# Attention written out for TensorE by groups of key tiles: the sample stream among the first head pair's blocks, and the first output-projection tiles in the last pair

## The chip, the core and the metric

The kernel runs on one core of a Trainium2 chip. The metric is the device time of one execution, in microseconds (us), as the median over runs. Five engines are named as the profile names them: PE (TensorE matmuls; PEld is its weight load), DVE (VectorE), ACT (ScalarE), POOL (GpSimd) and SP (SyncE, which issues the DMA transfers here). Each engine works through its own instructions in the order in which the program put them and waits on semaphores for the others.

## What is computed

Two layers over one prompt of 1024 tokens and a sample stream of 64 tokens with 512 cached keys. Only layer 0 matters here. Its even mixer takes one combined input projection and one output projection around two branches:

```
q, k, v, ga, qi, ki, wi, gb, gc, xin, gz = split(h @ w_in)
score = sum_h wi * relu(qi . ki)                    # the indexer
top_idx = top_k(score, min(256, L // 4))            # per query
p = softmax(q . k[top_idx] / 8);  o = p . v[top_idx]
a_out = o * silu(ga)                                # branch A
b_out = gb * conv3(gc * xin) * silu(gz)             # branch B
x = x + gate * (concat(a_out, b_out) @ w_out)
```

The kernel doesn't gather: a search finds each query's threshold score, a mask turns it into a bias that is added to the logits of all keys, and the softmax runs over all keys of a block.

## The kernel before

**Matmuls.** Every fp32 product is made of three: each operand is split into a high part (`hi`) and a rest (`lo`), and hi x hi, lo x hi, hi x lo are summed. A weight tile of the input projection (128 output channels) takes 8 slices of the inner dimension x 3 products x 3 column chunks (364, 364, 360 of the 1088 tokens), 72 matmuls, here called **steps**: `steps` (L250, its matmul is L262) is a generator that hands out one at a time. Weights come by SP (`w_raw`), ACT makes `w_hi` (L238), and POOL, or for the output projection mostly DVE, makes `w_lo` (L239).

**Masks.** Once the thresholds are known, DVE makes the bias of seven blocks (`mask`, L602 to L607) while PE works on the projection tiles that are still left: 11 of them, `ATTN_TILES` (queries of pairs 1 to 3, `gb` 0 to 3, `ga` 0 to 3). Their results are taken out of PSUM by ACT, and those of `gb` by DVE (L894), which multiplies them into `bo`.

**Attention.** Four head pairs `t`, each with eight blocks `b` of 128 queries (block b sees 128(b+1) keys) and then a sample block (64 queries of both heads in one, 576 keys). One block: logits on PE (L620), a masked maximum on DVE that also moves them to SBUF as `S` (L622), exp and sum on ACT (L625), reciprocal on DVE (L626), scaling on POOL (L627), transposes of `S` on PE by groups of two key tiles x two heads (L650), a split of these into `pth` (ACT, L276) and `ptl` (DVE, L277), and the weighted sum of v on PE (L658). ACT and DVE bring the result into `q` (L662, L722). At a pair's start ACT and POOL split its queries into `qst` (L698, L699). After a pair POOL multiplies `q` by silu(ga) (L912); for pair 3, ACT and DVE do it by chunks (L905, L906).

**What sets the order.** The tile framework orders the instructions of each engine by its own simulated timeline. Into it the kernel ties the projection steps: `BEFORE = 435` steps come ahead of attention, and `pace` drops one or two more behind each logits, weighted-sum and transpose piece (`RATE`). PSUM has eight banks of 512 columns: two for projections (`pj`), three for logits (`lg`), two for transposes (`pt`), one for weighted sums (`av`).

**After attention** the output projection (op, L247) runs over three column chunks x eight tiles of `wo`; it needs `q` and `bo` split into `ah` and `al` (L276, L277), and adds into `x` (loaded by SP).

Of the kernel before, what the change touches and what calls it, by code (L numbers as in the profile page):

```python
# [9 lines left out]
F32 = mybir.dt.float32  # L10
# [7 lines left out]
P = 128  # L18
# [30 lines left out]
ATTN_TILES = [(Q_, 1), (Q_, 2), (Q_, 3), *((GB, t) for t in range(4)), *((GA, t) for t in range(4))]  # L49
# [35 lines left out]
ORDER = [(0, 1, 2, 3, 4, 5, 6, 7)] + [(7, 0, 6, 1, 5, 2, 4, 3)] * 3  # L85


BEFORE = 435
RATE = ((1, 1, 2),) * 4
# [8 lines left out]
class Trunk:  # L98
    def __init__(self, tc, ins, outs):
        self.tc, self.nc = tc, tc.nc  # L100
        self.i, self.o = ins, outs
        self.tags = ["pj"]

# [6 lines left out]
    def bank(self, tag, name):  # L110

        return self.ps.tile([P, 512], F32, tag=tag, name=name, bufs={"pj": 2, "lg": 3, "pt": 2, "av": 1}[tag])
# [137 lines left out]
    def steps(self, w, evac, chunks=range(NCH), n=2, tag="pj"):  # L250
# [3 lines left out]
        for c in chunks:  # L254
            a, b = CHUNKS[c]
            ps = self.bank(tag, "pj")[:, 0:b - a]
# [230 lines left out]
    def topk(self, pool):  # L487
# [11 lines left out]
        self.kneg = kneg = t("kneg")  # L499
# [11 lines left out]
        cv, m, sgn, limx, T, cand, flag = (t(n) for n in ("cv", "m", "sgn", "limx", "T", "cand", "flag"))  # L511
        self.T, self.cv, self.sgn = T, cv, sgn
        junks = [self.cum, pool.tile([P, SEQ], BF, name="junk")]
# [78 lines left out]
    def mask(self, pool, j):  # L592
# [14 lines left out]
        V.tensor_scalar(bi, bi, MASK, None, op0=OP.mult)  # L607


    def softmax(self, slot, lhs, keys, g, n, bias):  # L610

        nc = self.nc
        k, w = cut(n)
        p = self.S[:, slot:slot + n]
        st = self.small.tile([P, 4], F32, tag="sm", name="sm", bufs=8)
        for c in range(k):
            s = slice(c * w, (c + 1) * w)
            pt = self.bank("lg", "logit_ps")
            for i in range(2):
                mm = nc.tensor.matmul(pt[:, 0:w], lhs, keys[i][:, g, s], start=i == 0, stop=i == 1)  # L620
            self.pace(mm.ins, self.rate[0])
            nc.vector.tensor_tensor_reduce(out=p[:, s], in0=pt[:, 0:w], in1=bias[:, s], scale=-0.125,  # L622
                                           scalar=st[:, c - 1:c] if c else 3.0e38, op0=OP.add, op1=OP.min,
                                           accum_out=st[:, c:c + 1])
        nc.scalar.activation(p, p, AF.Exp, scale=-1.0, bias=st[:, k - 1:k], accum_out=st[:, 2:3])  # L625
        nc.vector.reciprocal(st[:, 3:4], st[:, 2:3])  # L626
        nc.gpsimd.tensor_scalar(p, p, st[:, 3:4], 0.0, op0=OP.mult, op1=OP.add)  # L627
        return p

    def weighted(self, pool, ps, g, n, vbase):  # L630

        nc = self.nc
        m = len(ps) * P
        av = self.bank("av", "av")
        nj = (n + P - 1) // P
        step = 512 // m
        for j0 in range(0, nj, step):
            js = range(j0, min(j0 + step, nj))
            full = [j for j in js if (j + 1) * P <= n]
            pt = self.bank("pt", "p_ps")  # L640
            hi = pool.tile([P, 512], F32R, tag="pth", name="pth", bufs=2)
            lo = pool.tile([P, 512], F32R, tag="ptl", name="ptl", bufs=2)
            for part in (full, [j for j in js if j not in full]):
                if not part:
                    continue
                r = min(P, n - part[0] * P)
                for j in part:
                    for i, p in enumerate(ps):
                        o = (j - j0) * m + i * P
                        mm = nc.tensor.transpose(pt[0:r, o:o + P], p[:, j * P:j * P + r], self.ident)  # L650
                if part is full:
                    self.pace(mm.ins, self.rate[2])
                x = slice((part[0] - j0) * m, (part[-1] + 1 - j0) * m)
                self.split(hi[0:r, x], lo[0:r, x], pt[0:r, x])
                for j in part:
                    o = (j - j0) * m
                    for i, t in enumerate((hi, lo)):
                        mm = nc.tensor.matmul(av[:, 0:m], self.vs[0:r, vbase + j, g, :], t[0:r, o:o + m],  # L658
                                              start=j == 0 and i == 0, stop=j == nj - 1 and i == 1)
            self.pace(mm.ins, self.rate[1])  # L660
        low = pool.tile([64, 256], F32, tag="avl", name="avl", bufs=2)
        nc.scalar.activation(low[:, 0:m], av[64:P, 0:m], AF.Copy)  # L662
        return av, low
# [27 lines left out]
    def pair_stack(self, pool, t):  # L691

        nc = self.nc
        st = [pool.tile([P, TC], F32R, tag=f"qst{e}", name="qst") for e in range(2)]
        for a, b in ((0, 512), (512, TC)):
            for e in range(2):
                x, h, l = self.q[64 * e:64 * e + 64, t, a:b], slice(64 * e, 64 * e + 64), slice(64 - 64 * e, P - 64 * e)
                nc.scalar.activation(st[e][h, a:b], x, AF.Copy)  # L698
                nc.gpsimd.tensor_sub(st[e][l, a:b], x, st[e][h, a:b])  # L699
        return st  # L700

    def sample_keys(self, pool):
        for g in range(2):
            for o in range(0, PAST, 256):
                raw = pool.tile([P, 256], F32, tag="ckr", name="ckr", bufs=1)
                self.load(raw, self.i["ck"][g, :, o:o + 256])
                self.split(self.kc[0][:, g, o:o + 256], self.kc[1][:, g, o:o + 256], raw, self.nc.gpsimd)
# [3 lines left out]
    def attend(self, pool, st, t, b):  # L711
        n = P * (b + 1)
        c = slice(b * P, (b + 1) * P)
        if b < 2:
            bias = self.corner[:, 256 - n:256]
        else:
            bias = self.bias[:, SOFF[b - 2]:SOFF[b - 2] + n]
        ps = [self.softmax(self.slot(n), st[e][:, c], self.kp, t // 2, n, bias) for e in range(2)]
        av, low = self.weighted(pool, ps, t // 2, n, 0)
        for e in range(2):  # L720
            s = slice(e * P, (e + 1) * P)
            self.nc.vector.tensor_add(self.q[64 * e:64 * e + 64, t, c], av[0:64, s], low[:, s])  # L722

    def attend_sample(self, pool, st, t):
        both = pool.tile([P, P], F32R, tag="qs", name="qs", bufs=1)
        for e in range(2):
            self.nc.vector.tensor_copy(both[:, e * DEC:(e + 1) * DEC], st[e][:, SO:SO + DEC])
# [34 lines left out]
    def layer0(self):  # L762
# [41 lines left out]
        with ExitStack() as es:  # L804
# [40 lines left out]
            with self.pool("search", "right") as se:  # L845
# [31 lines left out]
                for j in range(NSB):  # L877
                    self.mask(se, j)
# [342 lines left out]
```

## Time and profile before

| | |
|---|---|
| three runs | 1160.75, 1156.42, 1159.66 us; median 1159.66 us |
| the profiled execution, its own time | 1157.27 us (span 1155.5 us) |
| PE busy | 1100.1 us, 95% of the span, mean granted clock 0.983 |
| DVE, ACT, POOL busy | 58%, 45%, 38% |
| first of the 11 attention-phase projection tiles on PE | 344.70 us |
| first logits matmul | 424.81 us |
| end of the 96th matmul of the output projection | 653.7 us |

How to read it: times of a view count from the span's start. The three runs lie within 0.4% of each other, and the profiled execution is at their lower end. [...]

### The profile page before, as it was taken

The page shows a single profiled execution, that of the slowest core. Times are in us where ns is not written, and L with a number is a line of the kernel's source. Part 1 is how long each engine was busy: PE and PEld are TensorE (multiplying, and loading weights), DVE is VectorE, ACT ScalarE, POOL GpSimd, SP SyncE. Part 2 cuts the span into 40 slices and gives each one's busy share as a digit, 9 for nine tenths or more (in the row PEclk, how much of TensorE's full clock was granted, in tenths as well). Part 3 has the DMA queues.
Part 4 walks back from the last instruction along what each step waited for, and adds up shares of the span by engine and source line. Part 5 has one row for each costly group of instructions (what it writes and reads, how often), then busy time and mean ns, then how long its engine had stood idle before and what let it go on. Part 6 is the DMA issues. An engine that isn't in the chain of part 4 may idle for free.

```text
span 1155.5 us, 18886 instructions
## 1 busy us (share of the span) xinstructions
PE 1100.1 (95%) x7255; PEld 1051.7 (91%) x7255; DVE 670.9 (58%) x1657; ACT 516.8 (45%) x976; POOL 442.6 (38%) x454
## 2 busy tenths in 40 slices
PE   4899999999999979999898999999999999999997
PEld 4789689999999968888797999999999999999996
DVE  5712799998886998776666424411186064247134
ACT  5233686856777147777757313511221211135111
POOL 2633223466547165354523136521133211154222
PEclk9999999999999989998999999999999999999999
DMA  9746411211101110000000801011112111131012
GB/s 362 305 156 215 179 29 56 91 40 38 37 19 56 37 46 10 20 1 19 19 1 19 281 2 40 35 55 37 37 57 82 37 37 37 38 109 37 1 65 91
DMA packets 26074, 81.84 MB, mean 71 GB/s; under 512 B 3072, under 2 KB 9984, under 8 KB 23552
## 3 DMA queue, kind: packets, MB, share of 16 engines
q1 hardware_dynamic: 25984, 80.63, 19.8%
q8 instruction: 57, 0.93, 0.3%
q14 instruction: 33, 0.27, 0.1%
HBM read 74.50 MB, written 6.12 MB: 70 GB/s over the span
## 4 chain that ended last, share of the span: by engine, by line
PE 79%; DVE 8%; ACT 5%; issue 3%; POOL 2%; DMA 2%; SPq 0%; POOLq 0%; DVEq 0%; ACTq 0%
PE pj L247 40%; PE op L247 16%; PE pj L262 8%; PE av L658 3%; PE p_ps L650 2%; PE logit_ps L620 2%; PE ada_ps L153 2%; PE score_ps L427 1%; PE sgu_ps L1036 1%; PE first L318 1%; DVE cum L604 1%; PE score_ps L428 1%; POOL w_lo L239 1%; POOL hf L329 1%; ACT S L625 1%
## 5 line engine op out<-in xcount | busy, mean ns | idle before, releaser
L247 PE MATMUL pj<-ah,w_hi 128*128 128x364 f32 (+1 forms) x984 | 326.0, 331 | 1.0 <-ACT w_hi L238 1.0
L247 PE MATMUL pj<-al,w_hi 128*128 128x364 f32 (+1 forms) x984 | 323.8, 329 | 0.0
L247 PE MATMUL pj<-ah,w_lo 128*128 128x364 f32 (+1 forms) x984 | 323.1, 329 | 0.0
L239 POOL TENSOR_TENSOR w_lo<-w_raw,w_hi 128x1024 fp32r<-128x1024 f32 x63 | 159.1, 2527 | 351.2 <-ACT w_hi L238 350.8
L247 PEld LDWEIGHTS pj<-ah,w_hi 128*128 128x128 f32 x984 | 185.0, 188 | 2.0 <-ACT w_hi L238 1.3
L247 PEld LDWEIGHTS pj<-ah,w_lo 128*128 128x128 f32 x984 | 184.8, 188 | 0.3 <-issue 0.2
L247 PEld LDWEIGHTS pj<-al,w_hi 128*128 128x128 f32 x984 | 185.1, 188 | 0.0
L238 ACT ACTIVATE w_hi<-w_raw 128x1024 fp32r<-128x1024 f32 x69 | 72.9, 1058 | 135.7 <-PE pj L247 83.2
L247 PE MATMUL op<-ah,w_lo 128*128 128x448 f32 (+2 forms) x384 | 126.5, 330 | 3.0 <-POOL w_lo L239 3.0
L247 PE MATMUL op<-ah,w_hi 128*128 128x448 f32 (+2 forms) x384 | 127.1, 331 | 0.9 <-ACT ah L276 0.5
L247 PE MATMUL op<-al,w_hi 128*128 128x448 f32 (+2 forms) x384 | 126.4, 329 | 0.7 <-DVE al L277 0.7
L528 DVE TENSOR_SCALAR_CACHE_REDUCE cum<-S,cand 128x512 bf16<-128x512 f32 (+5 forms) x142 | 119.1, 838 | 2.0
L262 PE MATMUL pj<-ah,w_hi 128*128 128x364 f32 (+1 forms) x288 | 96.0, 333 | 6.6 <-DVE bo L894 5.6
L262 PE MATMUL pj<-al,w_hi 128*128 128x364 f32 (+1 forms) x288 | 96.4, 335 | 0.0
L262 PE MATMUL pj<-ah,w_lo 128*128 128x364 f32 (+1 forms) x288 | 95.7, 332 | 0.0
L976 DVE SCALAR_TENSOR_TENSOR x<-op,mod,x 128x192 f32<-128x192 f32 (+2 forms) x64 | 30.4, 497 | 104.9 <-PE op L247 102.5
L555 ACT ACTIVATE junk<-S,cand 128x896 bf16<-128x896 f32 (+2 forms) x78 | 77.7, 996 | 24.3 <-DVE m L558 20.5
L627 POOL TENSOR_SCALAR S<-S,sm 128x384 f32<-128x384 f32 (+8 forms) x68 | 50.4, 748 | 87.2 <-DVE sm L626 64.9
L247 PEld LDWEIGHTS op<-ah,w_lo 128*128 128x128 f32 x384 | 73.0, 190 | 5.5 <-POOL w_lo L239 3.3
L247 PEld LDWEIGHTS op<-ah,w_hi 128*128 128x128 f32 x384 | 73.0, 190 | 3.5 <-ACT ah L276 0.9
L247 PEld LDWEIGHTS op<-al,w_hi 128*128 128x128 f32 x384 | 73.0, 190 | 3.3 <-DVE al L277 1.1
L984 POOL TENSOR_TENSOR acc<-acc,sq 128x448 f32<-128x448 f32 (+2 forms) x40 | 39.2, 979 | 94.4 <-ACT sq L982 93.6
(242 smaller groups left out, 2001.3 us busy)
## 6 DMA issues: line engine op xcount, KB each, us to landing
w_raw<-in_w SPq DMA_DIRECT2D x53, 512.0 KB, 3.4
ada<-in_ada_w SPq DMA_DIRECT2D x19, 1024.0 KB, 9.1
w_raw<-in_wo SPq DMA_DIRECT2D x16, 512.0 KB, 3.5
x<-in_x SPq DMA_DIRECT2D x8, 544.0 KB, 6.6
bo<-in_ada_w SPq DMA_DIRECT2D x4, 1024.0 KB, 6.9
x<-in_x SPq DMA_DIRECT2D x1, 1792.0 KB, 9.5
out_y<-x SPq DMA_DIRECT2D x1, 1792.0 KB, 6.6
x<-in_x SPq DMA_DIRECT2D x1, 1536.0 KB, 9.4
```

The source lines that it names most:

```text
L153: nc.tensor.matmul(pt[32 * g:32 * g + 32, 0:P], self.cs[:, kt, :], raw(kt)[:, g * P:(g + 1) * P], start=kt == 0, stop=kt == KT - 1, tile_p ...
L238: nc.scalar.activation(hi, raw, AF.Copy)
L239: (nc.gpsimd if lo_eng == "pool" else nc.vector).tensor_sub(lo, raw, hi)
L247: last = self.nc.tensor.matmul(ps, wt[:, kt, :], at[:, kt, c0:c1], start=n == 0, stop=n == len(mms) - 1)
L262: self.nc.tensor.matmul(ps, wt[:, kt, :], at[:, kt, a:b], start=kt == 0 and i == 0, stop=kt == KT - 1 and i == 2)
L528: V.tensor_scalar(junks[0][:, 0:SW[j]], self.S[:, span(j)], thr, 0.0, op0=OP.is_lt, op1=OP.add, accum_out=col(cv, j))
L555: nc.scalar.activation(junks[1][:, 0:SW[j]], self.S[:, span(j)], AF.Sign, scale=-1.0, bias=col(cand, j), accum_out=col(cv, j))
L620: mm = nc.tensor.matmul(pt[:, 0:w], lhs, keys[i][:, g, s], start=i == 0, stop=i == 1)
L627: nc.gpsimd.tensor_scalar(p, p, st[:, 3:4], 0.0, op0=OP.mult, op1=OP.add)
L658: mm = nc.tensor.matmul(av[:, 0:m], self.vs[0:r, vbase + j, g, :], t[0:r, o:o + m], start=j == 0 and i == 0, stop=j == nj - 1 and i == 1)
L976: nc.vector.scalar_tensor_tensor(x[:, t, a:b], ps[:, a:b], self.mod[l][:, 16 + t, j:j + 1], x[:, t, a:b], op0=OP.mult, op1=OP.add)
L984: nc.gpsimd.tensor_add(acc, acc, sq)
```

## The change

PE's order in the attention phase is no longer left to the framework: within `manual_schedule` for PE it is the program's own order. `attend` writes it out by **slots**; a slot is one group of two key tiles (four for a sample block), 88 in all. Each slot issues the transposes of its group, the logits of whatever block falls due (a block's last logits come `LEAD = 4` slots ahead of its first transposes), some projection steps (`FILL`: 2.9, 5.0, 5.5, 6.0 per slot in pairs 0 to 3, and 3.6 once the output projection has begun), and the weighted sum of the group two slots back (`LAG = 2`). The same matmuls are issued as before, in another order.

Besides:

- The four sample blocks stand among pair 0's blocks. All of pair 3's blocks but four then lie behind `half()`, from which on the slots are filled with the output projection's tiles 0 and 1 of chunk 0 (48 matmuls, `early_out`).
- `BEFORE` is 459. Ahead of attention the projection's results rotate over five banks instead of two; in attention `lg` has two banks, and weighted sums have two (`av` and `x`).
- The masks are emitted in the attention pool, and the scratch `cum` of `mask` shares the buffer of `ga`.
- silu(ga) is made as ga x (1 + tanh(ga/2)) with the half in the softmax's scale: tanh on ACT by chunks, a product on DVE, and a multiplication into `q` at the end of the pair (POOL; DVE for pair 3).
- The next pair's queries are split in the middle of the pair before; the sample keys and both sample query tiles ahead of attention.
- The output projection takes its inner slices in the order 4 to 7, 0 to 3 in layer 0.

```diff
+FILL = (2.9, 5.0, 5.5, 6.0, 3.6)
+LEAD, LAG = 4, 2
-ORDER = [(0, 1, 2, 3, 4, 5, 6, 7)] + [(7, 0, 6, 1, 5, 2, 4, 3)] * 3
-BEFORE = 435
-RATE = ((1, 1, 2),) * 4
+ORDER = [(0, 1, 2, 3, "s0", "s1", 6, "s2", "s3", 7, 5, 4)] + [(0, 7, 1, 6, 2, 5, 3, 4)] * 2 + [(0, 3, 1, 2, 4, 7, 5, 6)]
+BEFORE = 459
+OUT_KTS = (4, 5, 6, 7, 0, 1, 2, 3)
...
+    def attend(self, pool, through, half):
...
+        for g in range(int(ahead[0][0]), len(slots) + LAG):
+            if 0 <= g < len(slots):
+                it, js = slots[g]
+                waiting.append((it, js, self.transposes(pool, it, js)))
...
+                if js[0] == 0 and it in ((0, ORDER[0][-3]), (1, ORDER[1][3]), (2, ORDER[2][3])):
+                    self.queries(pool, it[0] + 1)
+            while ahead and ahead[0][0] <= g and self.room(ahead[0][1:]):
+                _, it, e, c = ahead.pop(0)
+                self.logits(it, e, c)
...
+            credit += FILL[-1 if self.halved else pair[min(max(g, 0), len(slots) - 1)]]
+            while credit >= 1:
+                credit -= 1
+                next(self.side, None)
+            if waiting and (len(waiting) > LAG or g >= len(slots)):
+                it, js, parts = waiting.pop(0)
+                self.weighted(pool, it, js, parts)
+                if (js[-1] + 1) * P >= self.keys_of(it):
+                    if it[1] == ORDER[it[0]][-1]:
+                        through(it[0])
+                    elif it == (3, ORDER[3][3]):
+                        half()
...
-                self.cum = se.tile([P, SEQ], BF, name="cum")
+                self.cum = ap.tile([P, 2 * TC], BF, tag="ga", name="cum")
...
+                        g = ga[t][:, cols(c)]
+                        nc.scalar.activation(g, ps, AF.Tanh, scale=0.5)
+                        nc.vector.scalar_tensor_tensor(g, g, 1.0, ps, op0=OP.add, op1=OP.mult)
...
-                        while kind == GA and self.done <= t:
+                        while kind == GA and not (self.last if t == 3 else self.done >= t):
                             yield
...
+                self.side = chain(tiles(), self.early_out(fetch))
+                self.tags = ["pj", "pj", "lg", "lg", "lg"]
+                with self.tc.manual_schedule(engines={mybir.EngineType.PE}):
+                    for j in range(NSB):
+                        self.mask(j)
+                    for _ in range(BEFORE):
+                        next(self.side)
+                    self.attending, self.tags = True, ["pj"]
+                    self.queries(ap, 0)
+                    self.sample_keys(ap)
+                    self.attend(ap, through, half)
```

Three places in the order show it. The first is DVE at the end of the masks (`bias`) and the start of attention (`S<-logit_ps`). Before, the last mask rows are mixed with results of `gb` (`bo`), and the first logits follow:

```order
L604 TENSOR_TENSOR_SCAN cum_1909<-ones_77,cv_1973,bias_600 128x576
L607 TENSOR_SCALAR bias_600<-bias_600 128x1024
L605 SCALAR_TENSOR_TENSOR bias_600<-cum_1909,bias_600 128x576
L894 TENSOR_TENSOR bo_604<-bo_604,pj_4385 128x364
L606 SCALAR_TENSOR_TENSOR bias_600<-S_603,T_1977,bias_600 128x576
L607 TENSOR_SCALAR bias_600<-bias_600 128x576
L894 TENSOR_TENSOR bo_604<-bo_604,pj_4411 128x360
L622 ISA S_603,sm_4457<-logit_ps_4458,corner_601 128x128
```

In the changed kernel the same place reads:

```order
L618 SCALAR_TENSOR_TENSOR cum_3874<-ones_77,cv_1909,bias_600 128x576
L983 TENSOR_TENSOR bo_604<-bo_604,pj_4381 128x364
L621 TENSOR_SCALAR bias_600<-bias_600 128x1024
L619 SCALAR_TENSOR_TENSOR bias_600<-cum_3874,bias_600 128x576
L620 SCALAR_TENSOR_TENSOR bias_600<-S_603,T_1911,bias_600 128x576
L983 TENSOR_TENSOR bo_604<-bo_604,pj_4407 128x360
L621 TENSOR_SCALAR bias_600<-bias_600 128x576
L997 SCALAR_TENSOR_TENSOR ga_4464<-ga_4464,pj_4439 128x364
L659 ISA S_603,sm_4501<-logit_ps_4502,corner_601 128x128
```

All masks still stand ahead of the first logits; new between them is the first product of `ga`, whose buffer `cum` has to leave first.

The second is PE at the end of pair 2. Before, the sample block's weighted sum (`av` of 128 columns) stands there with the next pair's logits and with two projection steps:

```order
L650 MATMUL p_ps_6258<-ident_69,S_603 128x128 x4
L262 MATMUL pj_6232<-al_65,w_hi_5642 128x364
L262 MATMUL pj_6232<-ah_64,w_lo_5643 128x364
L658 MATMUL av_6182<-pth_6184,vs_1905 128x128
...
L620 MATMUL logit_ps_6511<-kp0_1903,qst_6213 128x384
L620 MATMUL logit_ps_6511<-kp1_1904,qst_6213 128x384
L658 MATMUL av_6182<-ptl_6202,vs_1905 128x128
L650 MATMUL p_ps_6274<-ident_69,S_603 128x128 x4
```

In the changed kernel pair 3's first logits (`st1`) stand in a slot like any other, with steps of the projection in each:

```order
L275 MATMUL pj_6132<-ah_64,w_lo_5393 128x360
L702 MATMUL av_6244<-pth_6162,vs_1905 128x256
L702 MATMUL av_6244<-ptl_6163,vs_1905 128x256
...
L684 MATMUL p_ps_6249<-ident_69,S_603 128x128 x4
L658 MATMUL logit_ps_6259<-kp0_1903,st1_5016 128x128
L658 MATMUL logit_ps_6259<-kp1_1904,st1_5016 128x128
L275 MATMUL pj_6272<-ah_64,w_hi_5896 128x364
L275 MATMUL pj_6272<-al_65,w_hi_5896 128x364
L275 MATMUL pj_6272<-ah_64,w_lo_5897 128x364
```

What moved is the sample block (now in pair 0) and the projection steps, which are spread over the slots.

The third is ACT at the end of attention, where the output projection's third and fourth weight tiles (`w_hi`) are made. Before, they stand behind the splits (`ah`) that follow the last sample block:

```order
L662 ACTIVATE avl_6794<-av_6768 64x128
L276 ACTIVATE ah_64<-q_602 128x384
L276 ACTIVATE ah_64<-q_602 128x256
L238 ACTIVATE w_hi_6958<-w_raw_6956 128x1024
L238 ACTIVATE w_hi_6964<-w_raw_6962 128x1024
```

In the changed kernel they stand behind the last block's result (`cs` now holds what `avl` held):

```order
L289 ACTIVATE pth_6892<-p_ps_6891 128x256
L707 ACTIVATE cs_81<-av_6886 64x256
L289 ACTIVATE ah_64<-q_602 128x384
L289 ACTIVATE ah_64<-q_602 128x256
L249 ACTIVATE w_hi_6972<-w_raw_6970 128x1024
L249 ACTIVATE w_hi_6978<-w_raw_6976 128x1024
```

What moved here is little: the third tile is still made behind the last splits, but tiles 0 and 1 of chunk 0 have been multiplied by then.

## Rows read from the trace of the kernel before

**Rows 1.** The page: busy time of each engine, share of the span.

```profile
PE 1100.1 (95%) x7255; PEld 1051.7 (91%) x7255; DVE 670.9 (58%) x1657; ACT 516.8 (45%) x976; POOL 442.6 (38%) x454
```

**Rows 2.** Windows: length, then busy us of PE, PEld, DVE, ACT, POOL; PE's clock.

```profile
344.70:653.70 309.00, 285.95 (x1735) 266.29 (x1734) 228.53 (x638) 192.36 (x399) 136.76 (x131) 0.95 0.11 36
350.00:400.00 50.00, 50.00 (x303) 50.00 (x302) 40.92 (x117) 24.66 (x45) 24.70 (x30) 1.00 0.15 51
412.00:416.00 4.00, 3.91 (x14) 3.92 (x15) 4.00 (x3) 0.00 (x0) 3.85 (x3) 0.57 0.08 29
424.80:440.00 15.20, 12.94 (x72) 11.13 (x70) 12.28 (x54) 13.63 (x36) 10.96 (x15) 0.89 0.17 53
566.00:583.00 17.00, 13.01 (x62) 11.32 (x61) 8.70 (x29) 11.90 (x25) 8.98 (x9) 0.70 0.10 32
583.00:611.00 28.00, 27.86 (x195) 26.89 (x195) 18.14 (x58) 16.98 (x39) 6.69 (x9) 1.00 0.00 1
611.00:644.00 33.00, 28.02 (x158) 25.59 (x157) 22.28 (x44) 21.73 (x45) 9.89 (x3) 0.95 0.30 104
```

**Rows 3.** Waits of PE, 344.7 to 653.7: total us, times, longest.

```profile
PE pj L262 <- DVE bo L894: 5.6, 2, 3.3
PE p_ps L650 <- DVE ptl L277: 5.1, 6, 3.7
PE logit_ps L620 <- DVE sm L622: 3.3, 4, 2.2
PE op L247 <- POOL w_lo L239: 3.0, 1, 3.0
```

**Rows 4.** Timeline of DVE in the mask phase: start, us, instruction.

```profile
391.50 0.62 DVE L606 SCALAR_TENSOR_TENSOR bias<-S,T,bias 128x384 bf16<-128x384 f32 x1
394.54 2.77 DVE L606 SCALAR_TENSOR_TENSOR bias<-S,T,bias 128x512 bf16<-128x512 f32 x1
...
402.58 0.29 DVE L607 TENSOR_SCALAR bias<-bias 128x640 bf16<-128x640 bf16 x1
...
407.04 2.49 DVE L607 TENSOR_SCALAR bias<-bias 128x768 bf16<-128x768 bf16 x1
...
424.85 0.31 DVE L607 TENSOR_SCALAR bias<-bias 128x576 bf16<-128x576 bf16 x1
```

**Rows 5.** Timeline of POOL in the mask phase.

```profile
393.89 2.87 POOL L239 TENSOR_TENSOR w_lo<-w_raw,w_hi 128x1024 fp32r<-128x1024 f32 x1 [9.58 <-ACT w_hi L238]
405.89 3.42 POOL L239 TENSOR_TENSOR w_lo<-w_raw,w_hi 128x1024 fp32r<-128x1024 f32 x1 [9.13 <-ACT w_hi L238]
409.39 8.92 POOL L699 TENSOR_TENSOR qst<-q,qst 64x512 fp32r<-64x512 f32 x4
```

**Rows 6.** Lines by form, POOL, 440 to 620: count, busy us, mean ns, idle before.

```profile
L239 POOL TENSOR_TENSOR w_lo<-w_raw,w_hi 128x1024 fp32r<-128x1024 f32 x4 | 9.5, 2386 | 10.8 <-ACT w_hi L238 10.7
L699 POOL TENSOR_TENSOR qst<-q,qst 64x512 fp32r<-64x512 f32 x6 | 7.7, 1285 | 3.6 <-DVE sm L626 2.2 <-ACT qst L698 1.1
```

**Rows 7.** Lines by form, the softmax's chain and the splits, 440 to 620.

```profile
L622 DVE CUSTOM_DVE_ANT_0 S<-logit_ps,bias,sm 128x512 f32<-128x512 f32 x8 | 6.0, 750 | 1.9 <-PE p_ps L650 1.6
L625 ACT ACTIVATE S<-S,sm 128x1024 f32<-128x1024 f32 x8 | 9.2, 1148 | 1.2 <-DVE sm L622 1.2
L626 DVE RECIPROCAL sm<-sm 128x1 f32<-128x1 f32 x57 | 9.0, 160 | 13.0 <-ACT S L625 12.5
L627 POOL TENSOR_SCALAR S<-S,sm 128x1024 f32<-128x1024 f32 x8 | 9.0, 1123 | 27.2 <-DVE sm L626 27.1
L662 ACT ACTIVATE avl<-av 64x256 f32<-64x256 f32 x30 | 11.4, 381 | 8.7 <-PE av L658 8.1
L722 DVE TENSOR_TENSOR q<-av,avl 64x128 f32<-64x128 f32 x60 | 16.8, 280 | 7.9 <-ACT avl L662 7.3
L238 ACT ACTIVATE w_hi<-w_raw 128x1024 fp32r<-128x1024 f32 x4 | 4.2, 1050 | 0.1
```

**Rows 8.** The page's DMA issues: count, KB each, median us to landing.

```profile
x<-in_x SPq DMA_DIRECT2D x1, 1792.0 KB, 9.5
```

More of the change, by code (lines that the diff above doesn't have):

```diff
@@ L248, in product, with steps @@
         return last.ins
[L250 removed]
+    def steps(self, w, evac, chunks=range(NCH), n=2, tag=None):
         hi, lo = w
@@ L612, in softmax, with keys_of, logits @@
+    def keys_of(self, it):
+        return NS if self.sample(it) else P * (it[1] + 1)
+    def logits(self, it, e, c):
         nc = self.nc
+        t, b = it
+        n = self.keys_of(it)
         k, w = cut(n)
[L614 to L630, printed above, removed]
+        if self.sample(it):
+            lhs, keys, bias = self.both[t], self.kc, self.bias[:, SOFF[-1]:SOFF[-1] + n]
+        else:
+            lhs, keys = self.st[t % 2][e][:, b * P:(b + 1) * P], self.kp
+            bias = self.corner[:, 256 - n:256] if b < 2 else self.bias[:, SOFF[b - 2]:SOFF[b - 2] + n]
@@ new lines, in logits @@
+        if c == 0:
+            o = self.live[it, e][0]
+            self.p[it, e] = self.S[:, o:o + n], self.small.tile([P, 4], F32, tag="sm", name="sm", bufs=8)
+        p, st = self.p[it, e]
+        s = slice(c * w, (c + 1) * w)
+        pt = self.bank("lg", "logit_ps")
+        for i in range(2):
+            nc.tensor.matmul(pt[:, 0:w], lhs, keys[i][:, t // 2, s], start=i == 0, stop=i == 1)
+        nc.vector.tensor_tensor_reduce(out=p[:, s], in0=pt[:, 0:w], in1=bias[:, s], scale=-0.125,
+                                       scalar=st[:, c - 1:c] if c else 3.0e38, op0=OP.add, op1=OP.min,
+                                       accum_out=st[:, c:c + 1])
@@ L635, in weighted @@
[L635 to L660, printed above, removed]
@@ new lines, in transposes, with weighted @@
+        return hi, lo
+    def weighted(self, pool, it, js, parts):
+        nc = self.nc
+        t, b = it
+        n = self.keys_of(it)
+        m, w, vbase, o = (P, DEC, 8, SO) if self.sample(it) else (2 * P, P, 0, b * P)
+        if js[0] == 0:
+            self.av = self.bank("av", "av")
+        av = self.av
+        for j in js:
+            r = min(P, n - j * P)
+            x = (j - js[0]) * m
+            for i, part in enumerate(parts):
+                nc.tensor.matmul(av[:, 0:m], self.vs[0:r, vbase + j, t // 2, :], part[0:r, x:x + m],
+                                 start=j == 0 and i == 0, stop=(j + 1) * P >= n and i == 1)
+        if (js[-1] + 1) * P >= n:
+            low = self.cs.rearrange("p k c -> p (k c)")[0:64, :]
+            nc.scalar.activation(low[:, 0:m], av[64:P, 0:m], AF.Copy)
+            for e in range(2):
+                s = slice(e * w, (e + 1) * w)
+                nc.vector.tensor_add(self.q[64 * e:64 * e + 64, t, o:o + w], av[0:64, s], low[:, s])
@@ L724, in attend_sample @@
[L724 to L727, printed above, removed]
-        p = self.softmax(self.slot(NS), both, self.kc, t // 2, NS, self.bias[:, SOFF[-1]:SOFF[-1] + NS])
-        av, low = self.weighted(pool, [p], t // 2, NS, 8)
-        for e in range(2):
-            s = slice(e * DEC, (e + 1) * DEC)
-            self.nc.vector.tensor_add(self.q[64 * e:64 * e + 64, t, SO:SO + DEC], av[0:64, s], low[:, s])
```

235 lines of the change are left out of this document (153 added, 82 removed).

## The prediction

> **What bounds the kernel now.** I read the page first. TensorE (PE) is busy for 95% of the span [rows 1], so whatever is gained must be PE time: idle that goes, or a clock that is granted higher. The change issues the same matmuls, so there is no work to save. By the order of both kernels, PE's list is the same up to the start of attention and again from the fourth output-projection tile of the first chunk; between them the kinds of work alternate nearly equally often (340 changes from one kind to another before, 342 after), so I take what a change of kind costs inside busy time as equal.
>
> Next I cut the stretch in which the order differs out of the windows: 344.70 to 653.70 [rows 2]. It lasts 309.00 us with PE busy for 285.95, so 23.05 us are idle; its granted clock is 0.95, so about 309.00 x 0.05 = 15.5 us are lost to the clock. Together **38.5 us** can be had there at the most. Two windows say what is normal: 350 to 400 runs 303 steps in 50.00 us at full clock, 0.165 us a step, and 583 to 611, in the middle of a pair, has 195 matmuls in 28 us with 0.14 us idle [rows 2]. So the order inside a pair is already tight, and the loss sits at the edges.
>
> The waits name them [rows 3]: 5.6 us at the end of the pre-attention steps, where PE waits for a projection bank that DVE's L894 hasn't emptied, since that operation stands in line behind the masks; 5.1 us for `ptl`, the longest of 3.7 at a pair's end; 3.3 us for logits banks; 3.0 us at the output projection. The windows show what such an idle does to the clock: 566 to 583, the end of pair 2, has 3.99 us idle and then a granted 0.70, so 17 x 0.30 = 5.1 us more are lost. After the wait in front of 412 the clock was 0.57, 1.7 us in four. The start of attention (424.8 to 440) lost 2.26 us idle and 1.7 us of clock; the tail (611 to 644) 4.98 us idle and 1.65 us of clock [rows 2].
>
> **What the change takes away.** The sample blocks, small pieces with a long chain behind few matmuls, leave the pair ends, where the next pair's logits now stand with projection steps around them. Pair ends' waits (`ptl`, part of `sm`) and the slow clock behind them should go. The five banks ahead of attention take away the bank wait of 5.6 us. Two output tiles fill pair 3's slots, so that the 3.0 us wait for `w_lo` is met earlier. I set all 38.5 us to zero and then charge what is left, place by place.
>
> **Start of attention: 9.1 us.** By the order, every mask row on DVE still stands ahead of the first logits reduction, with one product of `ga` between. PE, now without bank waits, reaches the logits after 459 steps: 344.7 + 459 x 0.165 = 420.4, with the odd gap 421. DVE ended its masks at 425.2 before [rows 4]. Will that hold? DVE operations beside a tensor-tensor operation on POOL were stretched: L606 on 512 columns took 2.77 us, where 384 columns took 0.62, and L607 on 768 columns 2.49, where 640 took 0.29; each began after a `w_lo` on POOL had begun and ended within 0.6 us of that one's end [rows 4, 5]. That is about 2.1 us lost for each `w_lo`, which alone takes 2.39 [rows 6], a ratio of 0.87. Before, POOL had two `w_lo` and four `qst` pieces there [rows 5]: 2 x 2.39 + 4 x 1.29 = 9.9 us. After, by the order, it has three `w_lo`, four query pieces, and the sample's keys and queries (estimated as one more `w_lo` and a little, from their columns): 3 x 2.39 + 5.1 + 2.7 = 15.0. The extra 5.1 us cost between nothing (if they fall beside operations that weren't stretched) and 5.1 x 0.87 = 4.4 us. The row nearest is the stretched one; I take 3.7, the masks then end at 428.9. The product of `ga` behind them waits for its tanh on ACT, which may start only when `cum` is free: about 1.2 us with two hops. So PE waits from 421 to 430.1, **9.1 us** (5 if nothing is stretched, 10.5 with 5.1 us in full). Everything behind that reduction on DVE, and ACT's first exp, waits along.
>
> [...]
>
> **Ramp: 3 us.** After such an idle the first slots have no chain in flight and the clock restarts low. Before, this lost 3.9 us in 15.2 [rows 2]; LEAD's four slots are filled with steps here, so I take 3 (1.5 to 5).
>
> **In the pairs: 1.5 us.** A slot has 14 to 17 matmuls, at 28/195 = 0.144 us each [rows 2] 2.0 to 2.4 us. A block's scaled `S` must be ready three slots after its last logits, 6.0 to 7.2 us. The chain for 1024 keys is 0.75 + 1.15 + 0.16 + 1.12 = 3.2 us [rows 7]; for both heads one behind the other, and with what else stands in the queues, 4.5 to 6. It fits, barely in pair 0, where slots carry fewer steps and DVE takes the samples as well. At the end of pair 1 about four slots have no step, because `ga` tile 2 waits for the pair to end. I charge 1.5 us (0 to 6).
>
> **Weight tile in the middle of pair 3: 2 us.** By the order, POOL has a `w_lo` of the output projection directly ahead of a scaling of 1024 keys that the transposes need; that is 2.39 us [rows 6] in a chain with about 1 to 2 us to spare. 2 us (0 to 4).
>
> **Tail: 4 us.** PE's last weighted sum is followed at once by tile 2, whose `w_hi` stands on ACT behind the last block's result and the splits of the gated `q`. From PE's end: 0.38 + 2 x 0.28 + two multiplications of about 0.5 + two splits of about 0.5 + 1.05 = 4.0 us [rows 7], and hops; a few matmuls cover some. Before, the same place waited 3.0 us for `w_lo` [rows 3] and lost 4.98 in all. 4 us (3 to 6).
>
> **Weights of tile 4: 1.5 us.** SP issues the load of `x` only when attention has left its buffer, and the fifth weight tile stands behind it on SP. The load of `x` takes 9.5 us [rows 8]; PE has the tiles 2 and 3, 48 matmuls, about 9.9 us, and the 4 us above, in which to hide it and the conversion of the weights. 1.5 us (0 to 4).
>
> **Clock at the tail: 1.7 us**, as behind the wait in front of 412 [rows 2], since 4 us idle are no shorter than that wait (0 to 5).
>
> The silu by tanh costs DVE one more product per chunk of `ga` and spares table loads on ACT; neither engine is near full over the pairs (18.1 and 17.0 of 28 us [rows 2]), so I set it to nothing, with pair 0, where DVE is fullest, as the place where it would show.
>
> **Sum.** 9.1 + 3 + 1.5 + 2 + 4 + 1.5 + 1.7 = 22.8 us, against 38.5 before: 15.7 us gained. The profiled execution took 1157.27 us, so I predict **1142 us**. That execution lies 2.4 us below the median of the runs shown, 1159.66, so against the median the gain would read as 18.
>
> **Rivals.** (1) *More is gained.* If the extra POOL work meets operations that don't yield, the start costs 5, the ramp 1.5, pair 3's weight tile and the tail's fifth tile nothing, the tail 3 and its clock 1: 10.5 to 12 us are left, 27 gained, about 1130. For it: PE ran 28 us of a pair with 0.14 idle [rows 2]. Against it: two stretched rows. (2) *The clock takes it back.* The order leaves short idles as before, one at the start (certain) and one where slots have no step. If each drops the clock for as long as at the pair ends of before, 5.1 us each [rows 2], two of them make 10 us: 1152, and with one more at the tail 1157, no gain to speak of. For it: the clock fell behind each idle of 3 us or more in the trace. Against it: in the pairs the matmuls never stop that long unless a chain is late. (3) *Slower: the chain is longer than the lead.* PE's order is now fixed, so a late `S` stops steps too, which the old order could have sent ahead. 36 items (32 blocks and four samples) each pass this point. If each is late by x us the pairs cost 36x: the gain of 15.7 is gone at x = 0.44, and at 0.6 the time is about 1163. For it: 4.5 to 6 us of chain against 6.0 to 7.2 of lead, with pair 0's DVE the fullest. Against it: only blocks of 896 and 1024 keys have the long chain, eight of 32 blocks.
>
> **Chances.** The forecast (1134 to 1149) 0.57, rival 1 0.20, rival 2 0.16, rival 3 0.07. The range reaches from the better rival's middle to that of the clock: 1129 to 1154; beyond lie about 0.06 below and 0.13 above. Below about 0.5%, 6 us, a difference can't be told from none here. Rival 2 gives half of its chance to 1151 and less, so faster has 0.57 + 0.20 + 0.07, same 0.09, slower 0.07.
>
> **What would show it.** Right: PE's first logits wait of about 9 us for DVE at 421, then no wait over 1 us before 600, and a clock of 1.00 in the pair ends; the stretch ends at about 638 instead of 653.7. The masks' end on DVE tells the contention: 428.9 forecast, 425 for rival 1. Wrong: waits `p_ps` on POOL's `S` in many slots (rival 3), or windows at 0.7 in pair 1 or 2 (rival 2). What would make the forecast wrong most easily is the start: it is the largest term, and it rests on two stretched rows.

## The result and the profile after

The changed kernel took 1143.85 us (median of four runs, 1142.24 to 1145.28), the kernel before 1159.10; the ratio is 0.987 with a 95% interval of 0.9847 to 0.9894. The forecast was 1142 in a range of 1129 to 1154. The profiled execution took 1143.44 us (span 1141.7). So the sum came out right; its terms did not. The experiments show that holding PE to the written order gained nothing on balance: it took some 8 us out of the short gaps between matmuls and lost as much again in waits and slow clock. Two slow executions, 1622.61 us among the six of e12 and 3736.06 us of the kernel before in the group of e9 to e11, are left out of the times and ratios below.

The page answers to [rows 1]: PE is busy for the same 95% of a shorter span, 12.7 us less for the same number of instructions.

```profile
span 1141.7 us, 18832 instructions
PE 1087.4 (95%) x7255; PEld 1047.0 (92%) x7255; DVE 678.4 (59%) x1661; ACT 510.8 (45%) x974; POOL 443.2 (39%) x460
```

The windows answer to [rows 2] (length; busy PE, PEld, DVE, ACT, POOL; PE's clock; then the DMA engines' share and GB/s, not used here). The first is the whole stretch in which the order differs: 294.60 us instead of 309.00.

```profile
344.50:639.10 294.60, 273.13 (x1734) 262.52 (x1733) 236.47 (x642) 185.43 (x396) 136.71 (x137) 0.96 0.10 35
...
420.90:440.00 19.10, 9.71 (x42) 7.85 (x42) 13.37 (x35) 8.01 (x20) 5.31 (x9) 0.73 0.08 27
440.00:484.00 44.00, 42.50 (x300) 39.90 (x300) 36.15 (x118) 34.51 (x78) 25.01 (x28) 1.00 0.04 13
484.00:584.00 100.00, 98.05 (x687) 95.96 (x686) 79.73 (x249) 75.08 (x170) 47.92 (x49) 1.00 0.06 17
584.00:600.00 16.00, 10.93 (x56) 9.48 (x55) 15.87 (x44) 12.05 (x28) 6.12 (x4) 0.84 0.01 2
600.00:620.00 20.00, 20.00 (x132) 19.31 (x132) 14.79 (x38) 11.64 (x22) 4.50 (x5) 0.95 0.07 27
620.00:639.10 19.10, 15.55 (x67) 13.75 (x66) 9.58 (x14) 7.01 (x11) 3.14 (x2) 0.82 0.46 166
```

The 100 us from 484 to 584, which hold the ends of pairs 0, 1 and 2, have 1.95 us idle at full clock. Before, windows like 566 to 583 stood at such ends with 3.99 us idle and a clock of 0.70 [rows 2]. The loss now stands in three places: the start, 584 to 600, and the tail. The waits of PE name them; they answer to [rows 3]:

```profile
PE logit_ps L658 <- DVE bo L983: 7.5, 1, 7.5
PE op L258 <- ACT w_hi L249: 3.5, 1, 3.5
PE logit_ps L658 <- DVE sm L659: 3.1, 4, 1.2
PE p_ps L684 <- DVE sm L664: 3.1, 3, 1.4
PE op L1084 <- DVE ga L997: 2.4, 1, 2.4
```

*The start.* PE's timeline shows the last step, then the wait (the number in brackets):

```profile
420.74 0.33 PE L275 MATMUL pj<-ah,w_lo 128*128 128x364 f32 x1
428.61 0.69 PE L658 MATMUL logit_ps<-kp,st 128*128 128x128 f32 x2 [7.55 <-DVE bo L983]
```

On DVE the mask rows are stretched again, other ones than in [rows 4] (L617 on four blocks takes 4.92 us, where the same rows took 1.81 before, at 385.7). Its timeline, and under it POOL's:

```profile
385.47 4.92 DVE L617 TENSOR_SCALAR bias<-S,T 128x384 bf16<-128x384 f32 x4
390.31 0.52 DVE L983 TENSOR_TENSOR bo<-bo,pj 128x364 f32<-128x364 f32 x1
390.76 3.86 DVE L617 TENSOR_SCALAR bias<-S,T 128x896 bf16<-128x896 f32 x3
...
428.03 0.52 DVE L983 TENSOR_TENSOR bo<-bo,pj 128x360 f32<-128x360 f32 x1
428.47 0.30 DVE L621 TENSOR_SCALAR bias<-bias 128x576 bf16<-128x576 bf16 x1
428.69 0.53 DVE L997 SCALAR_TENSOR_TENSOR ga<-ga,pj 128x364 f32<-128x364 f32 x1
429.33 0.29 DVE L659 CUSTOM_DVE_ANT_0 S<-logit_ps,corner 128x128 f32<-128x128 f32 x1
```

```profile
384.17 5.80 POOL L747 TENSOR_TENSOR st<-q,st 64x512 fp32r<-64x512 f32 x4
390.05 0.92 POOL L747 TENSOR_TENSOR qs<-q,qs 64x64 fp32r<-64x64 f32 x2
391.04 3.26 POOL L290 TENSOR_TENSOR kc<-ckr,kc 128x512 fp32r<-128x512 f32 x2
```

The masks end at 428.77; 428.9 was forecast. But what lets PE go is not the first reduction: it is the last result of `gb`, which stands on DVE between two mask rows and holds a PSUM bank that the logits want. PE goes on at 428.6, 1.5 us earlier than forecast.

### The profile page after: what moved, and what is told of

Its sections match the earlier page's. It is cut to its first block, busy times and chain, and to the rows that moved or that the text cites. A ratio compares the mean times of both kernels' runs of the same rounds, so it can differ in the third digit from the quotient of the medians.

```text
span 1141.7 us, 18832 instructions
## 1 busy us (share of the span) xinstructions
PE 1087.4 (95%) x7255; PEld 1047.0 (92%) x7255; DVE 678.4 (59%) x1661; ACT 510.8 (45%) x974; POOL 443.2 (39%) x460
## 4 chain that ended last, share of the span: by engine, by line
PE 54%; DVE 4%; issue 1%; ACT 1%; DMA 1%; POOL 1%; POOLq 0%; DVEq 0%; ACTq 0%
PE pj L258 23%; PE op L258 15%; PE pj L275 4%; PE av L702 3%; PE p_ps L684 3%; PE logit_ps L658 2%; DVE al L290 2%; PE sgu_ps L1165 1%; PE op L1084 1%; DVE S L659 1%; DMA w_raw<-in_wo 1%; PE v_ps L1211 1%; POOL w_lo L250 1%; DVE ptl L290 0%; PE rstd L225 0%
## 5 line engine op out<-in xcount | busy, mean ns | idle before, releaser
L258 PE MATMUL op<-ah,w_hi 128*128 128x384 f32 (+2 forms) x368 | 122.1, 332 | 3.5 <-ACT w_hi L249 3.5
L258 PE MATMUL op<-al,w_hi 128*128 128x384 f32 (+2 forms) x368 | 121.3, 330 | 0.8 <-DVE al L290 0.8
L258 PE MATMUL op<-ah,w_lo 128*128 128x384 f32 (+2 forms) x368 | 120.4, 329 | 0.0
L542 DVE TENSOR_SCALAR_CACHE_REDUCE junk<-S,cand 128x512 bf16<-128x512 f32 (+5 forms) x142 | 119.0, 838 | 2.0
L665 POOL TENSOR_SCALAR S<-S,sm 128x128 f32<-128x128 f32 (+8 forms) x68 | 51.7, 764 | 90.9 <-DVE sm L664 74.2
L258 PEld LDWEIGHTS op<-ah,w_hi 128*128 128x128 f32 x368 | 70.4, 191 | 6.2 <-ACT w_hi L249 4.2
L258 PEld LDWEIGHTS op<-al,w_hi 128*128 128x128 f32 x368 | 70.5, 191 | 3.1 <-DVE al L290 1.1
L258 PEld LDWEIGHTS op<-ah,w_lo 128*128 128x128 f32 x368 | 70.3, 191 | 2.0
```

The lines of the kernel that those rows point to most:

```text
L258: last = self.nc.tensor.matmul(ps, wt[:, kt, :], at[:, kt, c0:c1], start=n == 0, stop=n == len(mms) - 1)
L542: V.tensor_scalar(junks[0][:, 0:SW[j]], self.S[:, span(j)], thr, 0.0, op0=OP.is_lt, op1=OP.add, accum_out=col(cv, j))
L665: nc.gpsimd.tensor_scalar(p, p, st[:, 3:4], 0.5, op0=OP.mult, op1=OP.mult)
```

## The experiments

All were timed beside the kernel before, on one chip per group. Medians in us:

| run | edit | median (range) | ratio to before (95%) |
|---|---|---|---|
| | the changed kernel | 1143.85 (1142.24 to 1145.28) | 0.987 (0.9847 to 0.9894) |
| e1_pool_quiet | POOL's splits in the mask phase left out | 1136.17 (1135.71 to 1136.59) | 0.9806 (0.9792 to 0.9821) |
| e2_before_banks5 | before, five banks ahead of attention | 1162.77 (1161.58 to 1165.58) | 1.0038 (1.0024 to 1.0051) |
| e3_lag1 | LAG 1 | 1146.55 (1145.20 to 1147.41) | 0.9895 (0.988 to 0.991) |
| e4_lead3 | LEAD 3 | 1147.35 (1147.11 to 1149.70) | 0.9908 (0.9892 to 0.9923) |
| e5_no_early | output tiles not written into the slots | 1145.24 (1143.43 to 1145.42) | 0.9881 (0.9861 to 0.9901) |
| e6_late_split | splits held back in pair 3 | 1144.37 (1142.29 to 1145.98) | 0.9871 (0.9844 to 0.9898) |
| e7_fill_tail | 2.6 steps per late slot | 1144.11 (1143.73 to 1145.13) | 0.9876 (0.9857 to 0.9896) |
| e8_before504 | 504 steps ahead of attention | 1135.43 (1135.23 to 1135.66) | 0.98 (0.9781 to 0.9819) |
| e9_framework | order left to the framework | 1142.26 (1142.07 to 1144.22) | 0.9859 (0.9836 to 0.9883) |
| e10_before_nosample | before, no sample attention | 1142.04 (1141.49 to 1143.98) | 0.9859 (0.9832 to 0.9887) |
| e11_before504_fill14 | e8 with 1.4 steps in pair 0 | 1136.36 (1135.00 to 1138.52) | 0.9806 (0.9782 to 0.9831) |
| e12_framework504 | e8 and e9 together | 1132.94 (1132.03 to 1133.76) | 0.9769 (0.9757 to 0.9782) |

### The start: e1, e2, e8, e11

```diff
+                    self.quiet = True          # e1, until attend's loop
...
+        if self.quiet:
+            nc.scalar.activation(lo, raw, AF.Copy)
```

> The changed kernel, but until attention's first logits POOL makes no second part of any split: three weight tiles, the queries of pair 0, the sample's queries and keys get theirs as a plain copy on ACT (their subtraction is left out). If POOL's operations stretch DVE's masks, the rows of the mask phase go back to their lone durations (L617 on four blocks 1.8 us in place of 4.92), the masks end 11 us earlier, at 418 instead of 428.8, PE hardly waits at the first logits, and the time falls by 9 to 13 us to 1131 to 1135. Rival: the masks are bound by DVE's own work and by the results of gb in between; then they end at 427 to 429 and the time is within 2 us of the changed kernel's.

The masks end at 420.45, 8.3 us earlier, and on DVE the L617 rows are no longer stretched: all seven take 3.74 us, where they took 8.78. PE doesn't stop (the same window as above):

```profile
420.90:440.00 19.10, 16.19 (x99) 13.75 (x98) 13.46 (x51) 15.28 (x39) 9.56 (x16) 1.00 0.01 5
```

So POOL's splits do stretch the masks. By the rows, the masks' operations took 11.0 us longer in the changed kernel than here (L617 5.0, two of L618 4.3, one of L621 1.7), the 11 that I had expected; their end moved by less, because DVE now stands 1.6 us in waits for PE and has one comparison of 1.3 us more behind the first L617. The whole gained 7.7 us, below the 9 that I had expected: this window went from 9.4 us idle to 2.9 and got its clock back, but 484 to 584 had 5.3 us idle, 3.3 more than in the changed kernel. DVE's rows lost 11.0 us beside 19.4 us of POOL's operations (384.2 to 421.8), a little over half. For the 5.1 us that I had estimated as added, the masks moved by 3.6, 0.7 of it; all of it would have had 430.3. Here too some rows were stretched and others not: beside the `w_lo` of 417.6, L618 on 1024 columns took 2.35 us, as in e1 (2.34), and L621 on 896 columns behind it 2.09 instead of 0.39.

```diff
...
+                self.tags = ["pj", "pj", "lg", "lg", "lg"]   # e2, in the kernel before
                 for _ in range(BEFORE):
                     next(self.side)
+                self.tags = ["pj"]
```

> The kernel before with one part of the change alone: ahead of attention its projection results rotate over five banks (two pj, three lg). If the start of attention is set by the end of DVE's masks, the waits of 5.6 us for L894 go and a wait of about the same size for DVE appears at the first logits; time within 2 us of before. Rival: the bank waits were the loss; then the 5.6 us and 1.7 us of clock are gained, about 1152.

It got slower by 3.7 us, which neither theory had. The bank waits went, and PE came to the first logits earlier: there it waited for the queries on POOL (until 424.9), and then for the bank that `bo` held (until 431.7):

```profile
PE logit_ps L622 <- POOL qst L701: 6.1, 2, 5.2
PE logit_ps L622 <- DVE bo L896: 5.7, 1, 5.7
```

Five banks alone gain nothing: they only let PE arrive earlier at a start that DVE and POOL set. That start isn't the same as before, though: the masks end at 431.8, 6.6 us later. They were 2.3 us late when the plain comparisons began; the other 4.3 came behind that, where POOL was at work from 420.2 on (a `w_lo` and the queries).

```diff
-BEFORE = 459
-FILL = (2.9, 5.0, 5.5, 6.0, 3.6)
+BEFORE = 504
+FILL = (2.2, 5.0, 5.5, 6.0, 3.6)
```

> The changed kernel with 45 more projection steps ahead of attention (504) and 2.2 instead of 2.9 per slot in pair 0. They are 7.4 us of work in the place of a wait of 7.5. If PE's wait at the start is plain loss, it goes, with most of the 5 us of clock around it: 6 to 11 us less, 1133 to 1138. Rival: pair 0 is bound by DVE (36 of 44 us busy at 440 to 484), the slots last as long with fewer steps in them and the gain is given back there; within 2 us of the changed kernel.

8.4 us less than the changed kernel; the wait is gone, at full clock. The windows from 420.9 on, as above:

```profile
420.90:440.00 19.10, 17.72 (x112) 16.51 (x111) 17.07 (x49) 12.33 (x32) 10.56 (x14) 1.00 0.16 56
440.00:484.00 44.00, 40.72 (x289) 37.88 (x288) 36.10 (x122) 34.47 (x76) 22.10 (x25) 1.00 0.00 1
484.00:584.00 100.00, 94.73 (x660) 91.82 (x659) 83.45 (x256) 77.41 (x178) 46.30 (x49) 1.00 0.05 17
584.00:600.00 16.00, 11.17 (x59) 10.28 (x58) 15.25 (x37) 9.02 (x18) 7.19 (x5) 0.79 0.10 34
```

About 5 of the 11 us that the start gave (8.0 idle and 3.0 of clock) are paid back from 440 to 584, where steps are missing now.

> The kernel with 504 steps ahead of attention, now with 1.4 steps per slot in pair 0 instead of 2.2, so that some 25 steps are left over for pair 1, whose slots ran out of steps (5.3 us idle at 484 to 584, against 2.0 in the changed kernel). If pair 0's slots are bound by DVE anyway, they last no longer with fewer steps, pair 1 is filled again, and 2 to 4 us are gained: 1131 to 1134. Rival: pair 0 opens gaps for what pair 1 closes; within 1.5 us of 1135.4.

The rival held in time, 0.9 us more than e8, but not in its cause: 484 to 584 lost 1.5 us less idle, 440 to 484 lost the same 3.3 as in e8, and new waits stand in pair 3, of `av` for DVE's `q` (4.0 us, at 582 to 590).

### The pairs: e3, e4, e9, e10

```diff
-LEAD, LAG = 4, 2
+LEAD, LAG = 4, 1      # e3;  e4 has 3, 2
```

> The changed kernel with weighted sums one slot behind their transposes instead of two. If the gain inside the pairs comes from splits that are ready long before PE wants them, short waits of av for pth and ptl come back, 0.05 to 0.1 us in each of 88 slots: 4 to 9 us slower than the changed kernel, 1148 to 1153. Rival: the lag plays no part, the filled slots do; within 2 us of the changed kernel.

2.7 us slower, and mostly not where I had said. Seven waits of the weighted sums for `ptl` and `pth` did come back (3.5 us), but the transposes' waits for `sm` and `ptl` went (4.3 us); 484 to 584 is as before (1.54 us idle), and the wait for `ga` at the first output matmuls grew from 2.4 to 6.5 us. The lag is not what takes the idle out of the pairs.

> The changed kernel with a block's logits three slots ahead of its first transposes instead of four. If the softmax chain nearly fills the lead (my third rival), the transposes wait in most of 36 items, 0.5 us or more each, at least 10 us in all, 1154 or more. If the lead has slack, only the 1024-key blocks wait, four or five times 1 us, 1146 to 1150.

3.5 us slower, with five waits for POOL's scaled `S` and not 36:

```profile
PE p_ps L684 <- POOL S L665: 8.3, 5, 3.1
```

So four slots of lead have slack for all but the longest blocks, and my third rival had little room.

```diff
-                with self.tc.manual_schedule(engines={mybir.EngineType.PE}):
+                if True:      # e9
```

> The changed kernel with the same program, but PE's order left to the framework's own timeline instead of written out. If the written order is what makes the pairs tight, the framework moves steps away from the places where they fill, waits of 1 us and more come back in the pairs and with them the slow clock: 8 to 15 us slower, 1152 to 1159. Rival: what counts is the rest (samples out of the pair ends, two transposed groups in flight, query splits ahead of time) and the order only follows it; within 3 us of the changed kernel.

The rival held: no slower, at most a little faster (the ranges overlap). The run takes away only the fixing of PE's order; the program that the framework starts from is still written in slots. The framework's order has a somewhat looser 484 to 584, but neither the waits at 584 to 600 nor the slow clock behind them: it sends the output matmuls from 581.0 on, beside DVE's splits, where the written order sends the first at 595.8.

```profile
484.00:584.00 100.00, 97.06 (x653) 89.23 (x653) 82.78 (x261) 79.54 (x182) 50.50 (x49) 1.00 0.04 12
584.00:600.00 16.00, 15.89 (x103) 13.91 (x102) 14.85 (x51) 11.49 (x29) 7.57 (x9) 1.00 0.09 33
```

```diff
-                    self.attend_sample(ap, st, t)      # e10, in the kernel before
```

> The kernel before with the four sample attention blocks left out (the sample's 64 tokens get no attention). Their matmuls are 8 to 9 us of PE. If it is the sample block that makes the pair ends idle and slow (6.2 us idle and 10.1 us of clock at the two late ones), the time falls by 15 to 24 us, to 1135 to 1144. Rival: the pair's end itself does it, since the next pair's queries and first logits come late whatever stands ahead of them; then it falls by the matmuls alone, to 1148 to 1152.

16 us less than the kernel before in its group. The matmuls left out are 16 logits of 288 columns, 40 weighted sums of 128 and 20 transposes, about 8 us by their median spacing at full clock in the trace of before; the other 8 went with them. In the traces the stretch of attention became 15.1 us shorter: 10.6 of busy time at full clock (the matmuls and the short gaps around them), 4.5 of clock, and no idle, 23.0 us in sum as before, since other waits grew (for POOL's `w_lo` at the output projection from 3.0 to 5.2 us). The two late pair ends, moved by the missing work:

```profile
510.00:530.00 20.00, 17.84 (x116) 16.19 (x114) 14.04 (x46) 16.89 (x34) 10.52 (x10) 0.91 0.08 27
555.00:575.00 20.00, 16.26 (x101) 14.62 (x100) 13.12 (x44) 15.14 (x32) 8.59 (x10) 0.91 0.08 27
```

They lose 4.0 and 5.5 us there (idle, and 9% of the window for the clock), 9.5 together, against 16.3 before (6.2 idle and 10.1 of clock, at 516 to 540 and 566 to 583). Both theories hold in part: the sample block makes some four tenths of the loss, what else stands at the pair's end the rest.

### The last pair and the tail: e5, e6, e7

```diff
-                self.side = chain(tiles(), self.early_out(fetch))
+                self.side = tiles()      # e5
...
```

> The changed kernel without the early output tiles: their 48 matmuls come after attention, as the others do, and pair 3's later slots carry no step. If the early tiles are worth what they fill, 14 slots each lose about 0.5 us to the chain, the waits at 584 to 600 stay, and the time is 5 to 8 us more, about 1150. Rival: they buy nothing, because tiles 0 and 1 behind attention would cover the 3.5 us wait and the 3.4 us of clock at the tail, and the splits they want on DVE make the waits of 5 us at 584 to 600; then the time is 1141 to 1146.

1.4 us more, with overlapping ranges, but the run doesn't tell the two theories apart: outside the written part the framework itself sent the output matmuls forward, and 48 of them again ran ahead of the last weighted sum, from 588.0 on in two lumps (9 did so in the kernel before). A wait took the place of those that they had covered:

```profile
PE p_ps L684 <- DVE ptl L290: 5.8, 4, 4.7
PE op L258 <- ACT w_hi L249: 3.5, 1, 3.5
```

It shows that it makes little difference who places them; what they are worth as such stays open.

```diff
...
+            it = (3, ORDER[3][4])
+            with self.tc.issue_after(self.lastcopy[it]), self.tc.issue_after(self.lastadd[it]):
                 for c in range(1, NCH):
...
                         self.out_split(c, k)
```

> The changed kernel with the splits of the output projection's second and third chunk held back on ACT and DVE until the fifth block of pair 3 is done (about 606). DVE is busy for 16.9 of 17 us at 583 to 600; if these splits in front of the softmax chain are the cause of the waits there (5.1 us, and 2.5 us of clock behind them), about half of both goes: 3 to 5 us less, 1139 to 1141. Rival: the chain is late there for another reason (the queue on POOL behind the multiplication by ga and a weight tile); then the waits stay and the tail grows by splits that are now late, 1144 to 1148.

No change. DVE has 3.2 us less to do at 584 to 600 and PE still loses 6.5 us there, and as much again where the splits went:

```profile
584.00:600.00 16.00, 12.88 (x64) 11.84 (x65) 12.70 (x35) 8.33 (x17) 5.86 (x5) 0.79 0.02 4
600.00:620.00 20.00, 16.55 (x94) 15.40 (x93) 15.58 (x40) 13.27 (x31) 3.41 (x4) 0.83 0.07 25
```

So the splits are not the cause by themselves: DVE and ACT have them to do somewhere in pair 3, and PE, in a fixed order, stops wherever they stand.

```diff
-FILL = (2.9, 5.0, 5.5, 6.0, 3.6)
+FILL = (2.9, 5.0, 5.5, 6.0, 2.6)
```

> The changed kernel with 2.6 instead of 3.6 steps per slot in pair 3's later part, so that about a dozen early output matmuls (2.5 us) are left to cover the wait for the third tile's weights at the end. If that wait and the clock behind it are plain loss, 3 to 5 us less, 1139 to 1141. Rival: the slots from 600 on are bound by ACT and DVE, a shorter fill only opens gaps there; within 1.5 us of the changed kernel.

The rival held. The slots from 600 to 620 opened (1.5 us idle and a clock of 0.91, where the changed kernel had none idle), and just ahead of them a weighted sum waited 3.0 us (until 599.8) for the bank that DVE's `q` empties, in place of the 2.4 us for `ga`. The wait for the third tile's weights stayed, 3.1 us.

### Together: e12

> Both findings together: PE's order left to the framework, 504 steps ahead of attention and 2.2 per slot in pair 0. If the two act in different places (the start, and pair 3's waits at 584 to 600, which the framework's order did not have), they add up: 1142.3 less about 8 to 10, 1132 to 1134. Rival: the framework had already moved steps to the start or takes the steps that are missing from pair 0 out of the later pairs; then no better than 1135.4.

1132.94 us, the fastest: 10.9 below the changed kernel, 26 below the kernel before. The start is filled, and the stall in the middle of pair 3 is small:

```profile
420.90:440.00 19.10, 18.57 (x114) 17.94 (x113) 13.86 (x32) 6.81 (x17) 5.76 (x7) 1.00 0.16 56
...
584.00:600.00 16.00, 15.29 (x97) 11.88 (x97) 15.46 (x50) 13.23 (x29) 7.17 (x7) 1.00 0.01 2
```

## Why the prediction was right, and where its steps were not

Summed over windows of 2 us, the stretch lost this much (idle plus clock; of the clock at the wait of 420.9 to 428.6, which costs nothing while PE stands, 2.1 us are left out):

| place | forecast | measured |
|---|---|---|
| wait at the start | 9.1 | 7.5 |
| ramp | 3 | 1.9 + 3.0 = 4.9 |
| in the pairs, 440 to 584 | 1.5 | 3.5 |
| weight tile in the middle of pair 3 (584 to 620) | 2 | 5.1 + 3.4 = 8.5 |
| tail: wait | 4 | 3.6 |
| weights of tile 4 | 1.5 | 0 |
| clock at the tail | 1.7 | 3.4 |
| sum, against 38.4 before | 22.8 | 31.4 |

By this the gain would have been 7 us; the stretch became 14.2 us shorter (by the starts of its first step and of the 97th output matmul, 308.8 before and 294.6 after), and the runs 15.3.

**Pair ends: right in place, in cause only in part.** Waits and slow clock at the ends of pairs 1 and 2 are gone, as forecast. e10 shows that the sample blocks made some four tenths of that loss. The trace of the kernel before names another part, the silu, which the prediction set to nothing. At the end of pair 2 it stands on ACT between two table loads, ahead of the exp and the split to which PE's longest wait goes back (ACT, then DVE, then PE):

```profile
568.29 1.28 ACT L911 ACT_TABLE_LOAD   x1
569.58 1.11 ACT L911 ACTIVATE ga<-ga 128x1088 f32<-128x1088 f32 x1
570.71 1.28 ACT L625 ACT_TABLE_LOAD   x1
572.01 1.04 ACT L625 ACTIVATE S<-S,sm 128x896 f32<-128x896 f32 x1
...
573.05 0.57 ACT L276 ACTIVATE pth<-p_ps 128x512 fp32r<-128x512 f32 x1
...
573.66 0.69 DVE L277 TENSOR_TENSOR ptl<-p_ps,pth 128x512 fp32r<-128x512 f32 x1 [0.32 <-ACT pth L276]
...
574.49 1.09 PE L650 MATMUL p_ps<-ident,S 128*128 128x128 f32 x4 [3.69 <-DVE ptl L277]
```

The two loads and the silu take 3.7 us of ACT there. At the end of pair 1 the loads stand at 518.7 and 522.2, and e10 keeps them at both ends. In the changed kernel, with tanh, the stretch has no table load behind the one at 427.8. No run changes the silu by itself, nor the queries split ahead, nor the next pair's logits spread over slots; how the remaining six tenths divide among these stays open.

**The start: right in place and cause, near in size.** The forecast wait of 9.1 at 421 was 7.5 at 420.9, and the ramp behind it 4.9 where 3 was charged; e1 shows POOL's splits behind 8.3 us of the masks' length, and e8 shows what the wait was worth, 8.4 us net. What ended it was a bank that `gb` held, not the first reduction.

**The middle of pair 3: mis-sized, by another mechanism.** I had charged 2 us for POOL's `w_lo` ahead of a scaling. It lost 8.5, in waits for DVE (1.4, 1.2 and 2.4 us) with DVE busy for 15.87 of 16 us; the prediction's own sign, no wait over 1 us before 600, was not met here. e6 shows that moving DVE's splits alone moves the stall; e9, with the same work in the framework's order, has 0.1 us idle there. That it is the earlier output matmuls which cover the splits is read from the order of the two traces and was not tried by itself.

**The step that failed:** "so I take what a change of kind costs inside busy time as equal". The number of changes of kind is the same, but about 7 us of the gain lie in gaps too short for the profile to call idle. The starts of all matmuls in the traces show where. From each stretch (first step to 97th output matmul) the table takes off the idle time and half of the time at the low clock while PE was busy (a granted 0.50, as at 413 to 415 before, where steps started 0.30 us apart; at full clock it is 0.165 [rows 2]); what is left are the same 1732 matmuls with the short gaps between them:

| kernel | PE's order | stretch | idle | clock | the rest |
|---|---|---|---|---|---|
| before | framework | 308.8 | 23.1 | 14.2 | 271.6 |
| changed | written | 294.6 | 21.5 | 9.0 | 264.2 |
| e9 | framework | 293.9 | 16.5 | 4.9 | 272.6 |
| e8, 504 steps | written | 287.6 | 18.5 | 4.0 | 265.1 |
| e12, 504 steps | framework | 284.8 | 9.4 | 1.7 | 273.8 |

The rest is 264 to 265 us in the written order and 272 to 274 in the framework's, with the same program in e9 as in the changed kernel. So it is the written order that shortens the gaps, by 8.4 us, and it pays 9.1 us for that in idle and clock. Against the median distance of two matmuls of the same kind and size, 6.3 of the 7.5 us between the kernel before and the changed one lie at the 342 changes of kind that each of them has: the step took as equal what was not. I first put these down to weighted sums that wait for splits just made; e3 gives 2.2 us of the rest back (266.4), 0.6 of it in 484 to 584, so the lag is a part of it at most. What shortens a change of kind in the written order stays open. This gain happened to cancel the mis-sized middle of pair 3; each alone would have missed the forecast by 7 to 9 us, still inside the range. The number was right by that luck.

**Rivals.** The better case needed a start without contention: that is e1, at 1136, not 1130. The clock's case came half true: slow stretches at the start, in pair 3 and at the tail, but none in pairs 1 and 2. The slower case had no room (e4).

## What to carry to other kernels

Find what the wait at a stage's start is worth by giving that time work from behind it: 45 steps moved ahead of attention gained 8.4 us, while fixing PE to the written order gained nothing on balance. Before an order is written out by hand, run the same program in the scheduler's order: here the rest of the change was the gain, and the fixed order paid for shorter gaps with a stall that the scheduler's did not have (5.1 us idle at 584 to 600, against 0.1). Before a side effect of a change is set to nothing, look at what it takes out of the queue that the longest wait goes back to: here the silu's table loads, two of 1.28 us, stood in it. Where idle and clock alone are summed, keep a term of both signs for gaps that the profile counts as busy.

## What the hardware showed that I had not expected

Not every DVE operation was stretched beside POOL: the threshold comparisons with an accumulator (L616; 1.20 us on 896 columns) took as long beside a `w_lo` on POOL as in e1 without one (1.20), while the plain comparisons behind them (L617, four blocks) took 4.92 beside the query splits, and 1.81 in the kernel before without these. POOL's operations were stretched as well: a `w_lo` took 4.17 us at 417.6 in the changed kernel, against a mean of 2.39 at 440 to 620 before [rows 6].
